# Sums of squares with the squares stationary, one pass for layer 0's two norms, and unsplit fp32 scores in layer 0's attention

## The chip, the cores and the metric

The kernel runs on one core of one Trainium2 chip. The metric is the device time of one execution in microseconds (us). Five engines work side by side: TensorE (PE in the profile, with its weight load PEld), VectorE (DVE), ScalarE (ACT), GpSimd (POOL) and SyncE (SP), which issues most transfers. The granted clock of TensorE (PEclk) is a share of full speed: 1.0 is 2.4 GHz, 0.5 is 1.2 GHz.

## The reference

Two blocks run one behind the other, on 256 tokens of 1024 features in fp32. The first has a state-space mixer, a sparse attention and a mixture of 32 experts, and ends with a norm. The second takes its result as x, has a context of 256 more tokens, and two layers: layer 0 with grouped-query attention (16 heads of 64 for queries, 4 for keys and values), layer 1 with latent attention. Each layer ends with a feed-forward part with a convolution. A norm divides a token by the root of its mean square; the shift and scale behind it come from a vector c ("ada" below):

```
def rms_norm(x, g):
    y = x * lax.rsqrt(jnp.mean(x * x, axis=-1, keepdims=True) + EPS)
    return y * g

def norm_modulate(h, g, shift, scale):
    return rms_norm(h, g) * (1 + scale) + shift
...
def attend(q, k, v):          # layer 0: keys of context and x, 512 in all
    s = jnp.einsum('bqhgd,bkhd->bhgqk', q, k) * scale
    p = softmax_f32(s)
    return jnp.einsum('bhgqk,bkhd->bqhgd', p, v)
```

Where the first block ends, two norms follow each other: x is normed by the block's last gain (final_g), and the result by layer 0's first norm.

## The kernel before

Activations lie feature-major: 128 features on the partitions, 8 tiles of them, 256 tokens along the free dimension. A projection (`lin_fm`, `lin_tm`) splits each fp32 weight into a high and a low part of type fp32r (ScalarE's cast L198, VectorE's difference L199) and makes three fp32r products of them (L217, L218, L219). An fp32r matmul is one record of TensorE in the trace, an fp32 matmul is two.

A norm of x or of the context (`rms_bcast`) has a chain. ScalarE squares two tiles at a time (L484). TensorE sums over features: 8 matmuls with 32 columns of ones stationary, the 256 squares moving, in the four column tiles of 32 (L489). VectorE copies the four partial sums to SBUF (L492), and two matmuls add them up, one column for each half of the tokens (L494). GpSimd takes the power of -1/2 (L507), VectorE puts it on a diagonal (L516), TensorE spreads it over the partitions (L519), VectorE and ScalarE make the scaled activation (L464, L465), which the next projection waits for. `rms_bcast` is called eight times: at the start of the first block; at about 483 us and 503 us for the context's first norm and the router's; at 670 us for the context's feed-forward part, at 1157 us for the context in layer 1; and for x at about 1191, 1407 and 1555 us.

`final_norm` stands where the first block ends (1014 us). It goes through `square_sums` twice, first with h, then with h times the gain (8 squares of ScalarE, L487), and gets the second norm from both (L1417).

In layer 0's attention for x, the queries (16 heads, two on the 128 partitions) and the keys are split into high and low parts as weights are: qTx, khi, klo. A score tile of one head and 128 queries is three fp32r matmuls of 64 rows with 512 keys (L1710); a pair of heads lies in the upper and lower 64 rows. Scores run two steps ahead of their use; between them stand the transposes of the probabilities (L1490) and the products with the values (L1498). VectorE takes the maxima (L1465), divides (L1480) and evicts transposes (L1492); ScalarE makes the exponentials (L1471).

The order of instructions is fixed when the program is built. Generators yield estimated costs, and `weave` and `mix` place a side chain's units among the main chain's by them; buffers of rings ("aux", "lin", "acc", "fl" are PSUM banks) and a planner then set the order on each engine. The ada columns of the second block (L391, `ada_quad`) are placed in this way beside the attention.

The PSUM tiles are called aux for sums of squares, transposes and spreads, lin for projections and scores; sq are squares, XA and the like scaled activations.

Of the kernel before, what the change touches and what calls it, by code (L numbers as in the profile page):

```python
# [88 lines left out]
# The experts by their rank in number of tokens: the order of the units (rank of group, half) and their blocks.  # L89
# [3 lines left out]
# The 8 KB buffers: those of the second part lie where what the first part keeps there is done early.  # L93
# [5 lines left out]
class Kernel:  # L99
# [21 lines left out]
    @contextmanager  # L121
    def banks(self, **bufs):
        """The eight PSUM banks, cut into rings for one part of the program."""
        with self.tc.tile_pool(name="psum", bufs=1, space=bass.MemoryType.PSUM, reuse_waits="tile") as self.psum:
            self.psum_bufs = bufs
            yield

    @contextmanager
    def phase(self, **bufs):
        """Buffers that live for one part of the program."""  # L130
        with self.tc.tile_pool(name="phase", bufs=1, reuse_waits="tile") as p:
            self.phase_pool, self.phase_bufs = p, bufs
# [37 lines left out]
    def passing(self, name, tag):  # L170
        """A constant that is needed only once."""
# [10 lines left out]
    # ---------------------------------------------------------------- weights  # L182
# [5 lines left out]
    def split_weight(self, view):  # L188
        """(hi, lo) of each block of 128 rows of a view [128, n, cols]."""
# [31 lines left out]
    def lin_fm(self, W, c0, ncols, act, evict, k0=0, nk=None, more=False):  # L221
        """out^T: features on partitions. W [K, N] in DRAM; act (hi, lo) [128, nk, 256]."""
# [24 lines left out]
    def lin_tm(self, W, c0, ncols, act, evict, chunk=512):  # L247
        """out: tokens on partitions."""
# [25 lines left out]
    # ---------------------------------------------------------------- set-up  # L274
# [73 lines left out]
    def load_fm(self, src, h, tag, eng):  # L348
        """[256, 1024] rows of DRAM -> feature-major h [128, 8, 256]."""
# [16 lines left out]
    # ---------------------------------------------------------------- adaLN  # L366
# [11 lines left out]
    def take_bias(self, stg, dst):  # L378
        """The bias into dst [128, slots, 48], to which the products are added."""
# [5 lines left out]
    def ada_quad(self, W, q, dst, rsel):  # L385
        """Columns 2048q..2048q+2047 of silu(c) @ W onto dst [128, slots, 48]."""
# [17 lines left out]
    def ada_start(self, p):  # L404
        """Shift and scale of the first norm for half of the features, in the order of ada1."""
# [70 lines left out]
    # ---------------------------------------------------------------- norms  # L476
    def square_sums(self, h, nt, st, gain=None):
        """Sums of squares over features (32 times them) into the two columns of st: the column tiles of TensorE add up
        a quarter each."""
        acc = self.ps("aux", [P, TOK])  # L480
        for k in range(0, nt, 2):
            sq = self.sb("k2", [P, 2, TOK], name="sq")
            if gain is None:
                self.A.activation(sq, h[:, k:k + 2, :], AF.Square)  # L484
            for i in range(2):
                if gain is not None:
                    self.A.activation(sq[:, i, :], h[:, k + i, :], AF.Square, scale=self.v(gain, k + i))  # L487
                c = (k + i) % 4
                self.T.matmul(acc[32 * c:32 * c + 32, :], self.ones[:, 0:32], sq[:, i, :], start=(k < 4),  # L489
                              stop=(k >= nt - 4), skip_group_check=True)  # L490
        part = self.sb("k1", [P, TOK], name="sqsum")
        self.V.tensor_copy(part, acc)  # L492
        for t in range(2):
            self.T.matmul(st[:, t:t + 1], part[:, t * P:t * P + P], self.ones[:, 0:1], start=(t == 0), stop=True,  # L494
                          skip_group_check=True)

    def rms_bcast(self, h, nt, dim):
        """1/rms over features, one column per token, on all partitions (PSUM [128, 256])."""
        st = self.ps("aux", [P, 2])
        self.square_sums(h, nt, st)  # L500
        return self.rstd_bcast(st, 2, 32 * dim)
# [8 lines left out]
    def spread(self, r, n):  # L510
        """Columns of r, one value per token, along the free dimension of all partitions."""
# [11 lines left out]
    def modulation(self, gain, ada, slot, vs, vsc):  # L523
        """gain * (1 + scale) and shift, [128, 8] each."""
# [15 lines left out]
    # ---------------------------------------------------------------- first block: projections  # L540
# [26 lines left out]
    def rope(self, x, nh, t, outs):  # L567
        """x [128, nh, 64] token-major, half-split rotation; written to each of outs."""
# [12 lines left out]
    def project_tm(self, act, pss):  # L581
        """dt, q, k/v, gates of the first block, tokens on partitions; the first two chunks are in pss."""
# [8 lines left out]
    def conv_silu(self, dst, ps, wname, bname, m, nm, taps):  # L591
        """Causal depthwise convolution over tokens, then silu."""
# [20 lines left out]
    # ---------------------------------------------------------------- SSD  # L613
# [40 lines left out]
    def ssd(self):  # L654
        """The chunked scan; y (with the skip) replaces the x channels. Yields where TensorE would wait."""
# [90 lines left out]
    def ssd_gate(self, act, sums):  # L746
        """y * silu(z), and its squares summed by group into sums [2][128, 2, 256]."""
# [35 lines left out]
    # ---------------------------------------------------------------- NSA  # L783
# [141 lines left out]
    def nsa_attend(self):  # L925
        """Selected and window branches (causal both: every block is chosen and the window spans the sequence)."""
# [85 lines left out]
    def tanh_gates(self, act, c0, sg):  # L1012
        """tanh(x / 2): the sigmoid is half of one more."""
# [78 lines left out]
    # ---------------------------------------------------------------- mixture of experts  # L1092
    def router(self, h):
# [35 lines left out]
        def top(x):  # L1129
            """softmax over the 8 columns; its sorted values and their places."""  # L1130
# [55 lines left out]
        # experts by their number of tokens: place of each expert and expert of each place  # L1186
# [67 lines left out]
    def one_hots(self, d, cols):  # L1254
        """For positions 256 d + cols: token x position, by first and second choice, [128, 2, n] per half of tokens."""
# [10 lines left out]
    def expert_gather(self, d, tag, n=256):  # L1266
        """The normalised tokens at positions 256 d.., features on partitions."""
# [15 lines left out]
    def expert_weights(self, part, experts):  # L1283
        """One part of the experts' weights, 256 rows of gate or up or 256 columns of down each."""
# [693 lines left out]
```

## Time and profile before

| what | value |
|---|---|
| runs, device us | 1765.72, 1766.47 (median), 1770.18 |
| profiled execution, span | 1765.9 us |
| TensorE busy | 1690.6 us (96%) |
| its weight load | 1379.4 us (78%) |
| VectorE busy | 1272.3 us (72%) |
| ScalarE busy | 917.8 us (52%) |
| GpSimd busy | 42.4 us (2%) |
| moved by DMA | 381.54 MB, 216 GB/s on average |

The span goes from the first to the last instruction of the profiled execution; no time around it is given apart, and the median of the runs lies 0.6 us above. Busy shares are means over the whole span; a stretch can look quite different. TensorE's ends are modelled: two matmul rows can overlap, and the pace of a row is the distance to the next row's start.

### The profile page before, as it was taken

Reading aid. Unit: us, or ns where it says so; the run is one execution under the profiler, and the core shown is the slowest. Engines: PE = TensorE matmul, PEld = TensorE weight load, DVE = VectorE, ACT = ScalarE, POOL = GpSimd, SP = SyncE. Lnnn points to the kernel's source line nnn. Section 1 sums busy time; section 2 is a strip of 40 time slices with the busy share of each in tenths; the row PEclk is TensorE's granted clock in tenths of the full one; section 3 lists DMA queues with packets and bytes.
Section 4 is the critical chain, followed back from the end, with each engine's and each line's share of the span. In section 5 each row is a group of like instructions: output and inputs, shape, how many; then the busy total and the mean of one; then the engine's idle time right before and its main releaser. Section 6 shows DMA issues by size and latency. Waiting matters only on the chain. (4 is left out here: it accounts for less than half of the span.)

```text
span 1765.9 us, 36466 instructions
## 1 busy us (share of the span) xinstructions
PE 1690.6 (96%) x12980; PEld 1379.4 (78%) x12980; DVE 1272.3 (72%) x3070; ACT 917.8 (52%) x1901; POOL 42.4 (2%) x48
## 2 busy tenths in 40 slices
PE   7999999999999999999999898999999989999998
PEld 3898777767876578888887554688999866789997
DVE  3997687675667768757756466968777788777876
ACT  2666446863443544534434252656665566556654
POOL 0000000100001000000000001000000000000000
PEclk8999999999999999999999988999999999999999
DMA  9756956849966997998999886234566432246662
GB/s 321 212 150 195 322 175 191 253 133 306 317 201 207 323 318 240 329 328 268 325 347 346 258 299 229 90 122 138 178 183 183 141 120 72 59 141 183 180 186 72
DMA packets 344962, 381.54 MB, mean 216 GB/s; under 512 B 27353, under 2 KB 298454, under 8 KB 344774
## 3 DMA queue, kind: packets, MB, share of 16 engines
q1 hardware_dynamic: 339456, 376.47, 67.2%
q10 hardware_dynamic: 5174, 1.97, 0.4%
q8 instruction: 104, 1.70, 0.4%
q0 software_dynamic: 144, 0.71, 0.1%
q14 instruction: 84, 0.69, 0.1%
HBM read 378.00 MB, written 1.05 MB: 215 GB/s over the span
## 5 line engine op out<-in xcount | busy, mean ns | idle before, releaser
L198 ACT CAST whi<-raw 128x512 fp32r<-128x512 f32 (+2 forms) x752 | 453.9, 610 | 383.9 <-PE lin L219 219.5
L199 DVE TENSOR_TENSOR wlo<-raw,whi 128x512 fp32r<-128x512 f32 (+2 forms) x752 | 502.4, 678 | 161.5 <-ACT whi L198 148.6
L217 PE MATMUL lin<-XA,whi 128*128 128x256 f32 x768 | 220.1, 287 | 1.7 <-ACT XA L465 1.7
L219 PE MATMUL lin<-XA,whi 128*128 128x256 f32 x768 | 219.0, 286 | 0.0
L218 PE MATMUL lin<-XA,wlo 128*128 128x256 f32 x768 | 218.9, 285 | 0.0
L217 PE MATMUL lin<-A,whi 128*128 128x256 f32 x576 | 168.4, 292 | 2.7 <-DVE k L598 1.9
L218 PE MATMUL lin<-A,wlo 128*128 128x256 f32 x576 | 163.5, 284 | 0.0
L217 PEld LDWEIGHTS lin<-XA,whi 128*128 128x128 f32 x768 | 149.3, 194 | 2.6 <-ACT XA L465 2.5
L218 PEld LDWEIGHTS lin<-XA,wlo 128*128 128x128 f32 x768 | 149.2, 194 | 0.7 <-issue 0.4
L219 PEld LDWEIGHTS lin<-XA,whi 128*128 128x128 f32 x768 | 148.9, 194 | 0.3
L217 PEld LDWEIGHTS lin<-A,whi 128*128 128x128 f32 x576 | 109.9, 191 | 33.8 <-issue 14.1
L219 PE MATMUL lin<-A,whi 128*128 128x256 f32 x448 | 127.7, 285 | 0.0
L217 PE MATMUL lin<-CA,whi 128*128 128x256 f32 x416 | 122.0, 293 | 0.3 <-ACT whi L198 0.2
L218 PE MATMUL lin<-CA,wlo 128*128 128x256 f32 x416 | 118.2, 284 | 1.1 <-DVE wlo L199 1.1
L219 PE MATMUL lin<-CA,whi 128*128 128x256 f32 x416 | 117.9, 283 | 0.0
L218 PEld LDWEIGHTS lin<-A,wlo 128*128 128x128 f32 x576 | 110.1, 191 | 0.9 <-issue 0.7
L1621 ACT ACTIVATE cv<-lin,vecs 128x256 f32<-128x256 f32 x132 | 73.9, 560 | 63.0 <-PE lin L219 52.7
L219 PE MATMUL lin<-XB,whi 128*128 128x256 f32 x352 | 99.4, 286 | 0.1
L1622 DVE SCALAR_TENSOR_TENSOR cv<-lin,vecs,cv 128x255 f32<-128x255 f32 x132 | 63.3, 480 | 49.4 <-ACT cv L1621 49.1
L217 PE MATMUL lin<-XB,whi 128*128 128x256 f32 x352 | 98.7, 283 | 0.0
L218 PE MATMUL lin<-XB,wlo 128*128 128x256 f32 x352 | 98.4, 283 | 0.0
L217 PEld LDWEIGHTS lin<-CA,whi 128*128 128x128 f32 x416 | 79.2, 190 | 15.5 <-issue 6.5
(534 smaller groups left out, 3835.0 us busy)
## 6 DMA issues: line engine op xcount, KB each, us to landing
raw<-in_ffn_w_up_dram SPq DMA_DIRECT2D x264, 256.0 KB
raw<-in_ada_w_dram SPq DMA_DIRECT2D x192, 256.0 KB
raw<-in_ffn_w_down_dram SPq DMA_DIRECT2D x132, 256.0 KB
raw<-in_w_in_dram SPq DMA_DIRECT2D x112, 256.0 KB
wx<-in_w_exp_gate_dram SPq DMA_DIRECT2D x112, 256.0 KB
wx<-in_w_exp_up_dram SPq DMA_DIRECT2D x112, 256.0 KB
wx<-in_w_exp_down_dram SPq DMA_DIRECT2D x112, 256.0 KB
raw<-in_w_ada_dram SPq DMA_DIRECT2D x96, 256.0 KB
```

The lines of the kernel that those rows point to most:

```text
L198: self.A.copy(hi, raw)
L199: self.V.tensor_tensor(lo, raw, hi.bitcast(F32), OP.subtract)
L217: mm(out, whi, ahi, start=first, stop=False, skip_group_check=True)
L218: mm(out, wlo, ahi, start=False, stop=False, skip_group_check=True)
L219: mm(out, whi, alo, start=False, stop=last, skip_group_check=True)
L1621: A.activation(acc, ps, AF.Identity, bias=self.v(f"fb{i}", m), scale=self.v(f"fw{i}1", m))
L1622: V.scalar_tensor_tensor(acc[:, 1:], ps[:, 0:TOK - 1], self.v(f"fw{i}0", m), acc[:, 1:], OP.mult, OP.add)
```

## The change

`square_sums` lets the squares be stationary: for each tile of features and each half of the tokens one fp32 matmul with 128x128 squares stationary and one or two columns of weights moving, all into one small PSUM tile. The copy (L492) and the two matmuls behind it (L494) are gone. `rms_bcast` takes ones as its one column.

`final_norm` makes one pass with two columns, gain squared plus EPS, and ones, and takes both norms from it. With s1 the mean of h squared and s2 the mean of h squared times gain squared, the second norm needs s2 + EPS (s1 + EPS): the first column's sum, with EPS squared added.

In layer 0's attention the queries and keys stay whole: the scores are one fp32 matmul each (`gqa_S`, which the context's attention had already), ScalarE evicts the queries' transposes, VectorE the keys'. The buffers khi, klo and the second qTx are gone. Comments and docstrings are gone too, so line numbers are lower in the changed kernel: L489 becomes L486, L519 L511, L1710 L1677 (in `gqa_S`), L1490 L1484, L1498 L1492.

```diff
-    def square_sums(self, h, nt, st, gain=None):
-        acc = self.ps("aux", [P, TOK])
-        for k in range(0, nt, 2):
+    def square_sums(self, h, weights, n):
+        st = self.ps("aux", [P, 2, n])
+        for k in range(0, 8, 2):
             sq = self.sb("k2", [P, 2, TOK], name="sq")
-            if gain is None:
-                self.A.activation(sq, h[:, k:k + 2, :], AF.Square)
+            self.A.activation(sq, h[:, k:k + 2, :], AF.Square)
             for i in range(2):
-                if gain is not None:
-                    self.A.activation(sq[:, i, :], h[:, k + i, :], AF.Square, scale=self.v(gain, k + i))
-                c = (k + i) % 4
-                self.T.matmul(acc[32 * c:32 * c + 32, :], self.ones[:, 0:32], sq[:, i, :], start=(k < 4),
-                              stop=(k >= nt - 4), skip_group_check=True)
-        part = self.sb("k1", [P, TOK], name="sqsum")
-        self.V.tensor_copy(part, acc)
-        for t in range(2):
-            self.T.matmul(st[:, t:t + 1], part[:, t * P:t * P + P], self.ones[:, 0:1], start=(t == 0), stop=True,
-                          skip_group_check=True)
+                for t in range(2):
+                    self.T.matmul(st[:, t, :], sq[:, i, t * P:t * P + P], weights(k + i), start=(k + i + t == 0),
+                                  stop=(k + i == 7), skip_group_check=True)
+        return st
...
     def rms_bcast(self, h, nt, dim):
-        st = self.ps("aux", [P, 2])
-        self.square_sums(h, nt, st)
-        return self.rstd_bcast(st, 2, 32 * dim)
+        st = self.square_sums(h, lambda k: self.ones[:, 0:1], 1)
+        return self.rstd_bcast(st.rearrange("p t n -> p (t n)"), 2, dim)
...
     def final_norm(self, h, gain, mod, tag):
-        count = 32 * D
-        st = [self.ps("aux", [P, 2]) for _ in range(2)]
-        self.square_sums(h, 8, st[0])
+        w = self.sb("s", [P, 8, 2])
+        V.tensor_tensor(w[:, :, 0], self.v(gain, 0, 8), self.v(gain, 0, 8), OP.mult)
+        V.tensor_scalar(w[:, :, 0], w[:, :, 0], EPS, None, OP.add)
+        V.memset(w[:, :, 1], 1.0)
+        st = self.square_sums(h, lambda k: w[:, k, :], 2)
         ms = self.sb("s", [P, 2, 2])
-        V.tensor_scalar(ms[:, 0, :], st[0], 1.0 / count, EPS, OP.mult, OP.add)
-        self.square_sums(h, 8, st[1], gain)
-        V.scalar_tensor_tensor(ms[:, 1, :], ms[:, 0, :], EPS * count, st[1], OP.mult, OP.add)
+        V.tensor_scalar(ms[:, 0, :], st[:, :, 0], 1.0 / D, EPS * EPS, OP.mult, OP.add)
...
         def take(t, c0, tp):
-            if not is_x:
...
-            elif c0 == 1024:
-                self.evict_split(*[k[:, :, TOK + t * P:TOK + t * P + P] for k in kT], tp)
+            if c0 == 1024:
+                k0 = (TOK if is_x else 0) + t * P
+                V.tensor_copy(kT[:, :, k0:k0 + P], tp)
             else:
-                self.evict_split(*[q[:, c0 // P:c0 // P + 4, t * P:t * P + P] for q in qT], tp)
+                A.copy(qT[:, c0 // P:c0 // P + 4, t * P:t * P + P], tp)
...
     def layer0_x_attend(self):
-        qT = [self.sb(n, [P, 8, TOK], F32R, name="qTx") for n in ("Q", "CA0")]
-        klo = self.sb("CA1", [P, 4, 512], F32R, name="klo")
...
-        def S_fn(S, i, t):
-            (qh, ql), (kh, kl) = [[x[:, i, t * P:t * P + P] for x in qT], [x[:, i // 2, :] for x in kT]]
-            for n, (q, k) in enumerate(((qh, kh), (ql, kh), (qh, kl))):
-                for a in range(2):
-                    r = slice(64 * a, 64 * a + 64)
-                    self.T.matmul(S[a], q[r], k[r], start=(n == 0), stop=(n == 2))
+        qT = self.sb("Q", [P, 8, TOK], name="qTx")
+        kT = self.kT2
+        S_fn = self.gqa_S(qT, 4)
```

At layer 0's two norms the order on TensorE was this in the kernel before (L489 the four column tiles' products, L494 their sums, L519 the spread, L391 products for ada, L217 and L218 projections):

```order
5004 L489 MATMUL aux<-sq,ones 32x256 x8
5005 L494 MATMUL aux<-ones,sqsum 128x1 x2
5006 L489 MATMUL aux<-sq,ones 32x256 x4
5007 L391 MATMUL fl<-raw,stat 32x512
5008 L489 MATMUL aux<-sq,ones 32x256 x4
5009 L391 MATMUL fl<-raw,stat 32x512 x2
5010 L494 MATMUL aux<-ones,sqsum 128x1 x2
5011 L391 MATMUL fl<-raw,stat 32x512
5012 L519 MATMUL aux<-k_14529,ones 128x256
5013 L391 MATMUL fl<-raw,stat 32x512 x2
5014 L217 MATMUL lin<-whi,XA_14533 128x512 x2
```

The first pass's sums stand between the two passes, and ada products among the second.

In the changed kernel the same place reads (L486 the new products, L511 the spread):

```order
5006 L486 MATMUL aux<-s,sq 128x2 x16
5007 L511 MATMUL aux<-k_14522,ones 128x256
5008 L391 MATMUL fl<-raw,stat 32x512
5009 L217 MATMUL lin<-whi,XA_14526 128x512 x2
5010 L391 MATMUL fl<-raw,stat 32x512
5011 L218 MATMUL lin<-whi,XA_14527 128x512
```

The two passes with ada products among them have become one run of 16 matmuls, and the ada products stand behind the spread.

In layer 0's attention, one period of the scores on TensorE before (L1490 transposes of probabilities, L1710 scores, L1498 and its second half products with the values):

```order
5203 L1490 MATMUL aux<-ident,prob 128x128 x8
5204 L1710 MATMUL lin<-khi,qTx 128x512 x4
5205 L1710 MATMUL lin<-klo,qTx 128x512 x2
5206 L1710 MATMUL lin<-khi,qTx 128x512 x2
5207 L1710 MATMUL lin<-klo,qTx 128x512
5208 L1490 MATMUL aux<-ident,prob 128x128 x8
5209 L1710 MATMUL lin<-khi,qTx 128x512 x2
5210 L1710 MATMUL lin<-klo,qTx 128x512
5211 L1498 MATMUL acc<-pT,vc 64x256 x4
5212 L1498 MATMUL acc<-pT,vx 64x256 x4
```

Four heads' scores stand in two places, three of them together.

And after (L1484 transposes, L1677 scores, L1492 products with the values):

```order
5200 L1484 MATMUL aux<-ident,prob 128x128 x8
5201 L1677 MATMUL lin<-kT_6574,qTx 128x512 x2
5202 L1484 MATMUL aux<-ident,prob 128x128 x8
5203 L1677 MATMUL lin<-kT_6574,qTx 128x512
5204 L1492 MATMUL acc<-pT,vc 64x256 x4
5205 L1492 MATMUL acc<-pT,vx 64x256 x4
5206 L1677 MATMUL lin<-kT_6574,qTx 128x512
5207 L1484 MATMUL aux<-ident,prob 128x128 x8
5208 L1677 MATMUL lin<-kT_6574,qTx 128x512 x2
5209 L391 MATMUL fl<-raw,stat 32x512 x3
```

Before, a period has the scores of a pair of heads, of a single head right behind it, and of another single head behind the next transposes; after, a pair and two single heads, one on each side of the products with the values.

## Rows read from the trace of the kernel before

**Rows 1.** Windows: us, busy time of PE, PEld, DVE, ACT, POOL, PEclk, DMA share, GB/s.

```profile
690.00:720.00 30.00, 30.00 (x287) 25.81 (x286) 21.35 (x47) 14.38 (x27) 0.00 (x0) 1.00 0.99 317
1011.00:1028.30 17.30, 12.76 (x52) 4.56 (x54) 5.33 (x15) 8.74 (x19) 1.66 (x2) 0.51 0.69 235
1108.66:1135.16 26.50, 26.50 (x177) 16.86 (x176) 25.56 (x65) 17.99 (x47) 0.00 (x0) 1.00 0.26 84
1560.00:1568.00 8.00, 6.89 (x33) 6.36 (x32) 6.62 (x16) 4.14 (x9) 0.00 (x0) 0.57 0.00 0
```

**Rows 2.** Time line of PE, router: start, us, line, out<-in, form, count.

```profile
517.67 2.20 PE L1114 MATMUL aux<-wr,hn 128*128 128x36 f32 x18
519.80 0.62 PE L391 MATMUL acc<-raw,stat 128*32 128x512 f32 x1
```

**Rows 3.** Time line of PE, the context's norm ahead of its feed-forward part.

```profile
670.13 1.07 PE L489 MATMUL aux<-sq,ones 128*32 128x256 f32 x16
671.13 1.13 PE L1317 MATMUL acc<-raw,xg 128*128 128x256 f32 x4
672.10 0.50 PE L494 MATMUL aux<-ones,sqsum 128*128 128x1 f32 x4
672.46 1.97 PE L1317 MATMUL acc<-raw,xg 128*128 128x256 f32 x8
```

**Rows 4.** Time line of PE, x's norm ahead of layer 1's feed-forward part.

```profile
1554.60 1.06 PE L489 MATMUL aux<-sq,ones 128*32 128x256 f32 x12
1556.30 0.63 PE L489 MATMUL aux<-sq,ones 128*32 128x256 f32 x4 [0.64 <-ACT sq L484]
1557.45 0.61 PE L494 MATMUL aux<-ones,sqsum 128*128 128x1 f32 x4 [0.53 <-DVE sqsum L492]
1559.73 0.67 PE L519 MATMUL aux<-k,ones 128*128 128x256 f32 x2 [1.67 <-DVE k L516]
```

**Rows 5.** Time line of PE, layer 0's two norms.

```profile
1014.88 2.62 PE L489 MATMUL aux<-sq,ones 128*32 128x256 f32 x16 [4.22 <-ACT sq L484]
1018.04 1.01 PE L494 MATMUL aux<-ones,sqsum 128*128 128x1 f32 x4 [0.53 <-DVE sqsum L492]
1018.98 1.08 PE L489 MATMUL aux<-sq,ones 128*32 128x256 f32 x8
...
1023.42 1.01 PE L494 MATMUL aux<-ones,sqsum 128*128 128x1 f32 x4
...
1028.83 0.50 PE L217 MATMUL lin<-whi,XA 128*128 128x512 f32 x1
```

**Rows 6.** Time line of PE, one period of layer 0's attention.

```profile
1118.18 0.73 PE L1710 MATMUL lin<-khi,qTx 64*128 64x512 f32 x4
...
1120.00 1.09 PE L1490 MATMUL aux<-ident,prob 128*128 128x128 f32 x8
1121.02 0.73 PE L1710 MATMUL lin<-khi,qTx 64*128 64x512 f32 x2
...
1121.91 0.44 PE L1498 MATMUL acc<-pT,vc 128*64 128x256 f32 x2
```

**Rows 7.** Time line of PE, fp32 scores of the first block.

```profile
336.41 1.13 PE L941 MATMUL S<-kT,qT 64*128 64x512 f32 x4
337.47 0.39 PE L217 MATMUL lin<-A,whi 128*128 128x256 f32 x1
```

**Rows 8.** Time line of PE, fp32 scores of the context's attention.

```profile
574.89 0.70 PE L1687 MATMUL S<-kT,qTc 64*128 64x256 f32 x4
...
599.56 0.70 PE L1687 MATMUL S<-kT,qTc 64*128 64x256 f32 x2
```

**Rows 9.** Time line of PE, projections and transposes ahead of layer 0's attention.

```profile
1064.02 0.39 PE L217 MATMUL lin<-whi,XA 128*128 128x512 f32 x1
1064.24 0.39 PE L218 MATMUL lin<-whi,XA 128*128 128x512 f32 x1
...
1067.91 0.63 PE L1571 MATMUL aux<-ident,pr 128*128 128x128 f32 x4 [2.08 <-DVE pr L1448]
```

More of the change, by code (lines that the diff above doesn't have):

```diff
@@ L1409, in final_norm @@
         a, b = mod
-        count = 32 * D
-        st = [self.ps("aux", [P, 2]) for _ in range(2)]
-        self.square_sums(h, 8, st[0])
+        w = self.sb("s", [P, 8, 2])
[3 more added lines that the diff above has]
+        st = self.square_sums(h, lambda k: w[:, k, :], 2)
         ms = self.sb("s", [P, 2, 2])
-        V.tensor_scalar(ms[:, 0, :], st[0], 1.0 / count, EPS, OP.mult, OP.add)
-        self.square_sums(h, 8, st[1], gain)
-        V.scalar_tensor_tensor(ms[:, 1, :], ms[:, 0, :], EPS * count, st[1], OP.mult, OP.add)
+        V.tensor_scalar(ms[:, 0, :], st[:, :, 0], 1.0 / D, EPS * EPS, OP.mult, OP.add)
         r = self.sb("s", [P, 2])
-        self.G.tensor_tensor(r, ms[:, 1, :], self.mhalf[:, 0:2], OP.pow)
+        self.G.tensor_tensor(r, ms[:, 0, :], self.mhalf[:, 0:2], OP.pow)
+        V.tensor_scalar(ms[:, 1, :], st[:, :, 1], 1.0 / D, EPS, OP.mult, OP.add)
         ag = self.sb("s", [P, 8])
-        V.scalar_tensor_tensor(ag, a, count ** 0.5, self.v(gain, 0, 8), OP.mult, OP.mult)
+        V.tensor_tensor(ag, a, self.v(gain, 0, 8), OP.mult)
         rb = self.spread(r, 2)
@@ L1425, in final_norm @@
         r1 = self.sb("s", [P, 2])
-        self.G.tensor_tensor(r1, ms[:, 0, :], self.mhalf[:, 0:2], OP.pow)
+        self.G.tensor_tensor(r1, ms[:, 1, :], self.mhalf[:, 0:2], OP.pow)
         def scale():
@@ L1586, in take @@
         def take(t, c0, tp):
-            if not is_x:
-                if c0 == 1024:
-                    V.tensor_copy(kT[:, :, t * P:t * P + P], tp)
-                else:
-                    A.copy(qT[:, c0 // P:c0 // P + 4, t * P:t * P + P], tp)
-            elif c0 == 1024:
-                self.evict_split(*[k[:, :, TOK + t * P:TOK + t * P + P] for k in kT], tp)
+            if c0 == 1024:
+                k0 = (TOK if is_x else 0) + t * P
+                V.tensor_copy(kT[:, :, k0:k0 + P], tp)
             else:
-                self.evict_split(*[q[:, c0 // P:c0 // P + 4, t * P:t * P + P] for q in qT], tp)
+                A.copy(qT[:, c0 // P:c0 // P + 4, t * P:t * P + P], tp)
         W = self.I["gqa_w_in_2"][0]
@@ L1692, in layer0_x_attend @@
         act, scale = self.final_norm(h, "final", self.mods(self.ada2[0], 0, "n1_0", 0), "XA")
-        qT = [self.sb(n, [P, 8, TOK], F32R, name="qTx") for n in ("Q", "CA0")]
-        klo = self.sb("CA1", [P, 4, 512], F32R, name="klo")
-        his = []
-        for g in range(0, 4, 2):
-            hi = self.sb("k2", [P, 2, TOK], F32R, name="khi")
-            self.evict_split(hi, klo[:, g:g + 2, 0:TOK], self.kT2[:, g:g + 2, 0:TOK])
-            his.append(hi)
-        khi = self.sb("K", [P, 4, 512], F32R, name="khi")
-        for g in range(0, 4, 2):
-            self.A.copy(khi[:, g:g + 2, 0:TOK], his[g // 2].bitcast(F32))
-        kT = khi, klo
-        def S_fn(S, i, t):
-            (qh, ql), (kh, kl) = [[x[:, i, t * P:t * P + P] for x in qT], [x[:, i // 2, :] for x in kT]]
-            for n, (q, k) in enumerate(((qh, kh), (ql, kh), (qh, kl))):
-                for a in range(2):
-                    r = slice(64 * a, 64 * a + 64)
-                    self.T.matmul(S[a], q[r], k[r], start=(n == 0), stop=(n == 2))
+        qT = self.sb("Q", [P, 8, TOK], name="qTx")
+        kT = self.kT2
+        S_fn = self.gqa_S(qT, 4)
         self.gqa_rope_tables()
```

## The prediction

> **What bounds the kernel now.** I read the stretches by engine first [rows 1], then the time line of TensorE where the change touches it, then the waits. In rows 1 the reader sees TensorE busy for all 30 us of 690 to 720 and all 26.5 us of the attention stretch 1108.66 to 1135.16. Two other engines stand close behind: the DMA engines are full in the first (share 0.99), VectorE in the second (25.56 of 26.50 us). So work added to TensorE shows in the end unless one of those two was late anyway. At the norms it is different: TensorE waits there, and afterwards the granted clock is low, 0.51 from 1011 to 1028.3 and 0.57 from 1560 to 1568 (most of it at 1.2 GHz, the rest at 2.4). There the chain from squares to the scaled activation sets the time.
>
> My sum is made against the profiled span, 1765.9 us. The median of the runs, 1766.47, lies 0.6 us above it, and I add that at the end. A change of less than 0.3% (5.3 us) can't be told from none.
>
> **The products of the norms.** Each call loses 8 matmuls with 32 stationary columns, one VectorE copy and two matmuls with the sum stationary. It gains 16 matmuls, each with its own 128x128 fp32 stationary and one or two moving columns. An fp32 matmul is two records. The nearest row is the router's product, 128x128 stationary and 36 moving columns: 18 records from 517.67, the next row starts at 519.80, so with its change-over 0.118 us a record [rows 2]. The 16 matmuls are 32 records: about 3.7 us at the full clock. What they replace is seen whole at the context's norm ahead of its feed-forward part: 1.00 us from 670.13 to 671.13, and 0.36 us from 672.10 to 672.46 [rows 3], 1.36 us in all. The four column tiles worked at once there. The price is +2.3 us of TensorE a call.
>
> The Trainium skill, "TensorE: Matmul & The Clock Gate", has two sections that price this differently. "Back-to-back issue gap" gives some 25 ns between matmuls of 1 to 64 columns; by that alone a call would be 0.8 us, cheaper than before (an estimate from the page). "LDWEIGHTS (loading the stationary operand)" gives columns over 1.2, thus 107 ns for 128 columns whatever the rows; by that a call is 3.4 us (an estimate too). The router's row, far above 25 ns, agrees with the second, and its 36 columns are no more than the first speaks of.
>
> Where does the +2.3 us count? Nine calls:
> - Four stand in full streams of TensorE (the context's first norm, the router's, the context's before its feed-forward part in layer 0, the context's in layer 1). Bounds: 0 each, if the transfers or a later wait take it up, and 2.3 each. The one at 670 stands right before the stretch with DMA share 0.99, so a later start there may be made up; the others have no such cover close behind. I take 1.3 each: +5.2, bounds 0 and +9.2.
> - Three are x's norms with TensorE waiting. In the one at 1554.60 the products waited for the last squares until 1556.30, then for the copy until 1557.45, and the last ended at 1557.45 + 0.61 = 1558.06 [rows 4]. The new ones run through: 1554.60 + 32 x 0.118 = 1558.38, with the end of the last about 0.1 later. The copy's wait of 0.53 and the squares' 0.64 are eaten by the backlog. +0.4 each, +1.2; bounds -0.6 each (if only the last pair of features is left when its squares come) and +1 each.
> - The first call lies where weights are still arriving: 0, bounds -0.5 and +0.5.
> - The last is the shared one of layer 0, below.
>
> **Layer 0's two norms.** Before, two passes go one behind the other: products from 1014.88, the sums of the first at 1018.04, the second's at 1023.42 + 1.01 = 1024.43, all at the low clock [rows 5]; then come the power on GpSimd, the spread and the first projection at 1028.83 [rows 5]. After, one pass of 32 records. At this clock the same kind of matmul takes 0.94 / 4 = 0.235 us a record (1018.04 to 1018.98) [rows 5]: 1014.88 + 7.5 = 1022.4, 2.0 us earlier. The eight scaled squares on ScalarE go too, and behind the power nothing changes. At the full clock 32 records would end 3.7 us earlier still; if the clock came back later because the stretch has less work in it, the gain would be 0. I take -2.0, bounds -5.7 and 0.
>
> **The scores of layer 0.** Before, a pair of heads is 6 records of fp32r, a single head 3. In one period of the attention there is a pair and a single from 1118.18 to 1120.00 and a single from 1121.02 to 1121.91: 1.82 + 0.89 = 2.71 us for four heads [rows 6]. Unsplit, a pair of 64-row heads with 512 keys is 4 records; the first block has the same shape in 1.06 us (336.41 to 337.47) [rows 7]. What one head alone costs is not in the trace with 512 keys; with 256 keys a single head lasts as long as a pair, 0.70 and 0.70 [rows 8], since the pair's row groups work side by side. So a single is 1.06 too. It now matters how the heads stand: the order puts pairs, and singles with other products between them. From the order's row 5183 on there are 24 heads in 7 pairs and 10 singles: 17 x 1.06 = 18.0 us. Before, 24 heads at 2.71 for four, the first pair at 0.9: 0.9 + 5.5 x 2.71 = 15.8 us. +2.2 us, bounds -3.1 (all 12 in pairs: 12.7) and +3.2 (another 0.1 for each change-over). TensorE was full there, so it counts. VectorE, at 25.56 of 26.50 us, loses nothing within that stretch, so it doesn't let the stretch get shorter either; it loses the low parts of q and k before it, 8 operations, and ScalarE as many. That lies beside TensorE's work and I count it at nothing; were it on the path, the q parts (two on the way to each four pairs of heads) could give back up to 1.4 us.
>
> **Moved.** The transposes of the first query heads stand behind 17 rather than 24 projections of the next chunk. Before, TensorE waited 2.08 us for them [rows 9]. Such a projection takes 0.22 us (1064.02 to 1064.24) [rows 9]; reached 7 of them earlier, 1.5 us, the transposes may wait as much longer, and what is behind them waits too; some of that is made up by the shorter norm ahead. +0.5, bounds 0 and +1.5. Before the attention is full, one head's scores now go ahead of 12 projections, and the softmax's start moves with them; the two sides about cancel: 0, bounds -2 and +2. The ada products that stand between them are the same in number.
>
> **Sum.** 5.2 + 1.2 + 0 - 2.0 + 2.2 + 0.5 = +7.1: a span of 1773.0, a median of 1773.6. I say 1773.5.
>
> **Rivals.**
> 1. The waits at the norms end and the clock stays up. In favour: the low clock after x's norm follows waits of 0.64, 0.53 and 1.67 us [rows 4], and the first two go. A mean of 0.57 over 8 us is 6.9 us at the lower level [rows 1], of which 3.4 would come back; for three such norms, taken as alike, 10.2, and 3.7 in the shared norm: 13.9, thus 1759.6, faster. It decides as soon as two stretches stay up and the shared norm runs at the full clock. Against it: from 1011 to 1028.3 TensorE worked 12.76 of 17.3 us and the clock stayed low [rows 1], so narrow work did not lift it there. Chance 0.15.
> 2. The additions are hidden. The four full calls are made up behind transfers and the scores stand as in the old order's bound: 7.1 - 5.2 - 1 = +0.9, thus 1767.4. For it: DMA share 0.99 and VectorE at 25.56 of 26.50 [rows 1]. Against: TensorE is busy 30.00 of 30 in the same rows, so nothing there stands idle to take it. Chance 0.30.
> 3. The products run at the pace of narrow matmuls, as if the load of the stationary cost nothing. (The Trainium skill, "TensorE: Matmul & The Clock Gate", "Back-to-back issue gap", would have them quicker still.) By rows: at the pace of the old ones, 16 records in 1.00 us [rows 3], 32 would be 2.0, +0.6 a call: 4 x 0.4 in the full streams, -0.6 at each of x's norms, -4.3 in the shared one (16 records took 2.62 us from 1014.88 [rows 5], so 32 end at 1020.1), +2.2 and +0.5: -1.8, thus 1764.7. Against: rows 2. Chance 0.05.
> 4. The clock falls more: 32 records of one column leave the array nearly empty, and each of x's three norms and the shared one has half as much time again at half speed (3.4 us, costing 1.7): +6.8, thus 1780.3. Chance 0.10.
>
> The forecast has 0.40. Below 1761.2 lies most of rival 1 (0.13); between 1761.2 and 1771.8 are rivals 2 and 3, the rest of rival 1 and the lower edge of the forecast (0.41); above, most of the forecast and rival 4 (0.46). The range runs from 1762 (both low bounds of full calls and scores: 1773.5 - 5.2 - 5.3 = 1763, and some of rival 1) to 1783 (9.2, the moved transposes at 1.5, and one more low clock stretch).
>
> **What would show it.** The new products at 0.12 us a record, 3.7 us a call: right; at 0.06 or less, rival 3. The single fp32 scores at 1.06: right; at 0.55, the scores gain. The first projection of layer 0 at about 2 us less after the products' start than the 13.95 us before. A granted clock of 1.0 after x's norms would be rival 1, and the time from 690 to 1011 growing shorter by what came before it, rival 2. I am wrong if the median is below 1771.8, and the sign is wrong below 1766.

## The result, and the profile after

The changed kernel takes 1786.5 us (median of 4 runs, 1783.98 to 1789.04), the kernel before in the same runs 1766.1. The ratio is 1.0108, 95% interval [1.0091, 1.0126]: 16 to 22 us slower, some 19 in the middle. I had forecast slower, by 7.1 us, with a range to 1783. So the sign was right and the size wrong by a factor of nearly three. The profiled execution has a span of 1787.3 us; the casts of the weights (L198) serve as marks along both traces, and the distance between them grows in four steps: 4.4 us by 100 us (an expectation below has it as 5.1), 10.4 by 660 us, 15.2 by 980 us, 20.6 to 21.4 from 1200 us to the end.

The time line of TensorE at the context's norm ahead of its feed-forward part answers to [rows 3], that at x's last norm to [rows 4], at layer 0's two norms to [rows 5] and in the attention to [rows 6]:

```profile
680.41 3.72 PE L486 MATMUL aux<-ones,sq 128*128 128x1 f32 x32
684.00 2.05 PE L1309 MATMUL acc<-raw,xg 128*128 128x256 f32 x4
...
1029.22 0.80 PE L486 MATMUL aux<-s,sq 128*128 128x2 f32 x3 [4.38 <-ACT sq L483]
1031.77 6.14 PE L486 MATMUL aux<-s,sq 128*128 128x2 f32 x29 [1.75 <-issue]
1039.58 1.19 PE L511 MATMUL aux<-k,ones 128*128 128x256 f32 x2 [1.68 <-DVE k L508]
1040.70 1.92 PE L391 MATMUL fl<-raw,stat 128*32 128x512 f32 x2
1042.55 1.22 PE L217 MATMUL lin<-whi,XA 128*128 128x512 f32 x2
...
1137.87 1.13 PE L1677 MATMUL lin<-kT,qTx 64*128 64x512 f32 x4
1138.93 1.09 PE L1484 MATMUL aux<-ident,prob 128*128 128x128 f32 x8
1139.96 1.12 PE L1677 MATMUL lin<-kT,qTx 64*128 64x512 f32 x2
1141.03 1.08 PE L1492 MATMUL acc<-pT,vc 128*64 128x256 f32 x8
...
1575.18 3.98 PE L486 MATMUL aux<-ones,sq 128*128 128x1 f32 x32
1580.83 1.19 PE L511 MATMUL aux<-k,ones 128*128 128x256 f32 x2 [1.67 <-DVE k L508]
```

The prices are as forecast. The 32 records take 684.00 - 680.41 = 3.59 us, 0.112 each, against 1.36 us for what they replace [rows 3]. A pair of heads takes 1138.93 - 1137.87 = 1.06 us, a single one 1141.03 - 1139.96 = 1.07. What was not in my sum at these norms stands behind the products. The windows give the time, the busy time of PE, PEld, DVE, ACT and POOL, the granted clock, the DMA share and GB/s; of each pair, the first ends with the products (at the context's first norm 16 of the 32 records, with projections among them) and the second is what follows:

```profile
489.60:492.80 3.20, 3.20 (x30) 3.20 (x30) 0.16 (x2) 0.62 (x1) 0.00 (x0) 1.00 0.66 244
492.80:496.20 3.40, 3.40 (x17) 3.22 (x16) 2.17 (x7) 1.15 (x2) 1.13 (x1) 0.51 0.29 78
...
680.40:684.00 3.60, 3.60 (x35) 3.60 (x33) 0.00 (x0) 1.62 (x3) 0.00 (x0) 1.00 0.00 0
684.00:687.40 3.40, 3.40 (x10) 2.53 (x10) 1.83 (x8) 0.00 (x0) 0.70 (x1) 0.50 0.07 9
```

TensorE is busy all through both pairs and waits for nothing, and yet the clock is at 1.2 GHz behind the products. In the kernel before it was at 2.4 GHz at these places:

```profile
480.00:500.00 20.00, 19.66 (x159) 17.51 (x158) 16.79 (x38) 12.37 (x24) 0.72 (x1) 1.00 0.61 204
500.00:520.00 20.00, 18.70 (x124) 12.16 (x123) 9.10 (x22) 7.18 (x15) 0.70 (x1) 1.00 0.58 171
660.00:680.00 20.00, 19.71 (x149) 17.67 (x148) 14.70 (x35) 7.65 (x16) 1.05 (x1) 1.00 0.59 187
```

The clock falls like this behind the context's first norm, with the router's last products (513 to 520 us), behind the context's norm before its feed-forward part, and once more in layer 1.

The two traces also tell where the scores cost: from the first product with the values to the last, TensorE needed 46.98 us before (the first two rows) and 51.27 after (the last two):

```profile
1108.66 0.65 PE L1498 MATMUL acc<-pT,vc 128*64 128x256 f32 x4
...
1155.64 1.24 PE L1498 MATMUL acc<-pT,vx 128*64 128x256 f32 x7
...
1120.51 1.08 PE L1492 MATMUL acc<-pT,vc 128*64 128x256 f32 x8
...
1171.78 1.24 PE L1492 MATMUL acc<-pT,vx 128*64 128x256 f32 x7
```

That is +4.3 us. By the distance of starts, the scores of the 22 heads in this stretch take 17.2 us for 14.0, and six records of ada products (L391), 1.0 us, stand inside it now, where there were none. But the first product with the values lay only 11.85 us behind the kernel before, 2.5 us less than at the first product of layer 0's norms (1014.88 to 1029.22, 14.3 us).

### The profile page after: what moved, and what is told of

Read it like the earlier page. It is cut to its first block, busy times and chain, and to the rows that moved or that the text cites. A ratio compares the mean times of both kernels' runs of the same rounds, so it can differ in the third digit from the quotient of the medians.

```text
span 1787.3 us, 36539 instructions
## 1 busy us (share of the span) xinstructions
PE 1716.0 (96%) x13036; PEld 1405.6 (79%) x13036; DVE 1267.3 (71%) x3057; ACT 912.9 (51%) x1887; POOL 42.0 (2%) x48
## 5 line engine op out<-in xcount | busy, mean ns | idle before, releaser
L198 ACT CAST whi<-raw 128x512 fp32r<-128x512 f32 (+2 forms) x752 | 454.0, 610 | 396.8 <-PE lin L219 228.0
L199 DVE TENSOR_TENSOR wlo<-raw,whi 128x512 fp32r<-128x512 f32 (+2 forms) x752 | 503.0, 679 | 168.0 <-ACT whi L198 153.0
L217 PE MATMUL lin<-XA,whi 128*128 128x256 f32 x768 | 220.0, 287 | 1.6 <-ACT XA L465 1.6
L218 PE MATMUL lin<-XA,wlo 128*128 128x256 f32 x768 | 218.8, 285 | 0.0
L217 PE MATMUL lin<-A,whi 128*128 128x256 f32 x576 | 168.4, 292 | 2.7 <-DVE k L590 1.9
L218 PE MATMUL lin<-A,wlo 128*128 128x256 f32 x576 | 163.5, 284 | 0.0
L217 PEld LDWEIGHTS lin<-XA,whi 128*128 128x128 f32 x768 | 149.3, 194 | 2.9 <-ACT XA L465 2.7
L218 PEld LDWEIGHTS lin<-XA,wlo 128*128 128x128 f32 x768 | 149.1, 194 | 0.6 <-issue 0.4
L217 PEld LDWEIGHTS lin<-A,whi 128*128 128x128 f32 x576 | 109.9, 191 | 33.8 <-issue 14.1
L217 PE MATMUL lin<-CA,whi 128*128 128x256 f32 x416 | 122.1, 294 | 0.2 <-ACT whi L198 0.2
L218 PE MATMUL lin<-CA,wlo 128*128 128x256 f32 x416 | 117.9, 283 | 1.1 <-DVE wlo L199 1.1
L218 PEld LDWEIGHTS lin<-A,wlo 128*128 128x128 f32 x576 | 110.1, 191 | 0.9 <-issue 0.7
L217 PE MATMUL lin<-XB,whi 128*128 128x256 f32 x352 | 98.7, 283 | 0.0
L218 PE MATMUL lin<-XB,wlo 128*128 128x256 f32 x352 | 98.4, 283 | 0.0
L217 PEld LDWEIGHTS lin<-CA,whi 128*128 128x128 f32 x416 | 79.3, 191 | 15.2 <-issue 7.0
```

Of the source, the lines that this page charges most:

```text
L198: self.A.copy(hi, raw)
L199: self.V.tensor_tensor(lo, raw, hi.bitcast(F32), OP.subtract)
L217: mm(out, whi, ahi, start=first, stop=False, skip_group_check=True)
L218: mm(out, wlo, ahi, start=False, stop=False, skip_group_check=True)
```

## The experiments

Each was timed in five rounds beside the kernel before, on one chip for each group of four or three kernels. A ratio is that to the kernel before, with its 95% interval, and microseconds are ratio minus one times its median (1767.5 to 1768.4 us in these runs).

**Scores or norms.** The first kernel is the kernel before with `layer0_x_attend` and `take` of the change, the second the kernel before with `square_sums`, `rms_bcast` and `final_norm` of the change.

> The kernel before with unsplit fp32 scores alone; all norms as before. Theory A (the new products of the norms make the loss): between 0 and +4 us against before, from +4.3 us in the full part of the attention and -2.4 us ahead of it, as the two traces differ there. Theory B (the scores are the main loss, by singles at 1.06 us and what they delay): +8 us or more.

> The kernel before with the new sums of squares in all nine calls and the shared pass; scores split as before. Theory A: +16 to +20 us, most of it at five calls in full streams (the first, the context's first, the router's, the context's two others), and a low granted clock after each of them. Theory B: +8 us or less.

Measured: 0.9996 [0.998, 1.0011] for the scores, -0.7 us; 1.0103 [1.0073, 1.0133] for the norms, +18 us. Within these intervals the whole loss is in the norms. In the scores' own trace the first product with the values starts at 1101.89, 6.8 us earlier than before, and the last at 1153.16, 2.5 us earlier: the +4.3 us inside the full attention is there again (as in all four profiles with unsplit scores), and made up ahead of it. What went ahead of it was not one wait: the transposes' 2.1 us [rows 9] and part of the low clock, which took 10.2 us from 1082.8 in the kernel before and 3.4 us at about that place here. The latter can't be put down to the scores: in the profiles of kernels that are as before in this part, that stretch is between 0 and 10.2 us long.

**Which norms.** `rms_bcast` takes the new sums in some of its calls only; the kernel with the shared norm has the change's `final_norm` instead:

```diff
     def rms_bcast(self, h, nt, dim):
+        self.calls = getattr(self, "calls", -1) + 1
+        if self.calls in (1, 2, 3, 4):      # (5, 6, 7) and (0,) in the others
+            st = self.square_sums_new(h, lambda k: self.ones[:, 0:1], 1)
+            return self.rstd_bcast(st.rearrange("p t n -> p (t n)"), 2, dim)
         st = self.ps("aux", [P, 2])
         self.square_sums(h, nt, st)
```

> The kernel before with the new sums of squares in four plain norms alone, those in TensorE's full streams (the context's first norm, the router's, the context's before its feed-forward part in layer 0, the context's in layer 1). Theory A (each costs 2.3 us of records, and the low clock behind it 1.7 us or more again): +11 to +15 us. Theory B (my prediction's price, 1.3 us each, the rest hidden): +5 us.

> The kernel before with the new sums of squares in x's three plain norms alone. Theory A: 0 to +2 us, since the products there run beside waits and the copy's chain goes. Rival: the low clock behind them gets longer, as in the changed kernel's trace (10.2 us in place of 6.8 at two of them), and they cost +3 us or more.

> The kernel before with the new sums of squares in the first norm alone (at 16 us). Theory A (its records on a full TensorE and the order that comes with it): +4 to +6 us, as the changed kernel lies 5.1 us behind by 100 us. Theory B (the start is bound by weights arriving, as I predicted): within 1 us of before.

> The kernel before with layer 0's two norms shared as in the change (squares stationary, two columns moving), nothing else. My prediction's term: -2.0 us, bounds -5.7 and 0. Rival from the changed kernel's trace, where the chain from the first square to the first projection took 14.0 us against 14.6: within 1 us of before.

| new sums in | ratio | interval | us |
|---|---|---|---|
| the four full streams | 1.0047 | [1.0033, 1.006] | +8.3 |
| x's three norms | 1.0013 | [1.0004, 1.0023] | +2.3 |
| the first norm | 1.004 | [1.0024, 1.0055] | +7.1 |
| layer 0's shared norm | 1.0012 | [1.0, 1.0023] | +2.1 |

The four add up to 19.8 us, the kernel with all of them had +18. So one call in nine, the first, costs nearly as much as the four in the full streams. These cost less than the +11 to +15 us that I expected then: the trace has +6.8 us behind the first two and another 3.3 us behind the third by 705 us, of which 1.0 is made up by 980 us and 4.1 more by 1150 us; the fourth adds 1.1 by 1190 us.

Why is the shared norm no gain? In this kernel its chain is shorter, as I forecast: 11.57 us from the first product to the first projection, where the ten profiles with the old norms and split scores here have 12.3 to 14.1. In its time line the last product of the experts starts at 1010.59, 0.90 us later than before, and the first projection 1.84 us earlier than [rows 5]:

```profile
1015.42 6.99 PE L506 MATMUL aux<-s,sq 128*128 128x2 f32 x32 [3.85 <-ACT sq L503]
1023.99 1.22 PE L535 MATMUL aux<-k,ones 128*128 128x256 f32 x2 [1.58 <-DVE k L532]
1025.13 1.92 PE L391 MATMUL fl<-raw,stat 128*32 128x512 f32 x4
1026.99 0.97 PE L217 MATMUL lin<-whi,XA 128*128 128x512 f32 x2
...
1078.51 0.73 PE L1729 MATMUL lin<-khi,qTx 64*128 64x512 f32 x4
```

But the first scores start at 1078.51, in the kernel before at 1078.34. The gain is gone in the projections: from the first of them to the first scores it is 51.5 us, and 48.2 to 50.4 in those ten. In the kernel before 12 records of ada products (L391) stood among the second pass, up to the first projection, and used its waits; here 4 stand ahead of it and the other 8 among the projections, where TensorE is full. Between the first projection and the first scores there are 60 such records now and 52 before; by the distance of starts they take 10.9 us for 9.2, and TensorE's waits there are 3.1 us for 2.3. That accounts for the gain in these two time lines; I didn't run a kernel that keeps the ada products back. In the changed kernel the chain gained less to begin with: TensorE stands still for 1.75 us behind the first three records (1029.22 and 1031.77 above), and the first projection comes 13.33 us behind the first product, against 13.95. What held it there the profile doesn't tell (`issue`).

**The low clock behind the products.** One norm alone (the context's in layer 1) takes the new sums, with 1, 36 and 128 columns of ones moving. TensorE's order is the same in the three, row by row.

```diff
-            st = self.square_sums_new(h, lambda k: self.ones[:, 0:1], 1)
-            return self.rstd_bcast(st.rearrange("p t n -> p (t n)"), 2, dim)
+            st = self.square_sums_new(h, lambda k: self.ones[:, 0:36], 36)
+            return self.rstd_bcast(st[:, :, 0], 2, dim)
```

> The kernel before with the new sums of squares in one plain norm alone, the context's in layer 1 (at 1157 us). Theory A: +2.3 us of records and 1.7 us for a stretch of low clock behind them: +3 to +5 us in the trace behind the norm. Theory B (records alone): +2.3 us.

> As the kernel with one new norm, with 36 columns of ones moving in place of one; TensorE's order is otherwise the same row by row. Theory A (the clock falls for the single column): the products take the same time, the granted clock stays at 1.0 behind them, and 1.7 us or more come back. Theory B: the same as with one column.

> As the kernel with one new norm (the context's in layer 1), with 128 columns of ones moving; TensorE's order is otherwise the same row by row. If the low clock behind the products comes from how little moves through TensorE, 128 columns keep it at 1.0 and the kernel is within 2 us of before plus the records' 2.3 us; if it comes from the stationary loads or from the stretch itself, the granted clock falls again right behind the products as with 1 and 36 columns.

Measured: 1.0019 [1.0006, 1.0032], 1.0016 [1.0004, 1.0028] and 1.0017 [1.0005, 1.003], so +3 us for each. The time lines of the products and, in the same order, the windows behind them:

```profile
1157.12 3.63 PE L506 MATMUL aux<-ones,sq 128*128 128x1 f32 x32
1160.61 0.36 PE L217 MATMUL lin<-CB,whi 128*128 128x256 f32 x1
```

```profile
1158.28 3.82 PE L506 MATMUL aux<-ones,sq 128*128 128x36 f32 x32
1161.91 0.56 PE L217 MATMUL lin<-CB,whi 128*128 128x256 f32 x1
```

```profile
1153.78 3.73 PE L506 MATMUL aux<-ones,sq 128*128 128x128 f32 x32
1157.27 0.36 PE L217 MATMUL lin<-CB,whi 128*128 128x256 f32 x1
```

```profile
1161.10:1164.50 3.40, 3.33 (x14) 2.89 (x14) 1.90 (x5) 0.03 (x1) 0.69 (x1) 0.51 0.13 38
```

```profile
1161.60:1165.00 3.40, 3.40 (x16) 3.17 (x15) 0.68 (x4) 0.00 (x0) 0.70 (x1) 0.50 0.07 24
```

```profile
1157.50:1161.00 3.50, 2.81 (x23) 2.58 (x22) 1.80 (x6) 0.67 (x2) 0.69 (x1) 1.00 0.00 1
```

The products take 3.49, 3.63 and 3.49 us, whatever moves: the loads of the stationary set their pace. Behind them the clock is low with 1 and with 36 columns and stays up with 128. So Theory A fell for 36 columns, and the time did not follow the clock here. In these profiles the low clock came earlier and not on top: with 128 columns, and in the kernel before, a stretch of 3.4 us begins later, at 1168.7 and 1171.6, behind a wait of TensorE for a weight's low part (L199) of 2.1 and 2.71 us, and with 1 and 36 columns there is none at that place, though TensorE waits 2.1 us there too. The windows of the kernel before, of that with 128 columns and of that with one (clock third from the end):

```profile
1172.00:1180.00 8.00, 8.00 (x57) 8.00 (x56) 3.71 (x8) 3.19 (x7) 0.00 (x0) 0.81 0.74 237
```

```profile
1165.00:1172.00 7.00, 4.68 (x24) 4.35 (x23) 5.95 (x13) 3.57 (x7) 0.00 (x0) 0.76 0.40 119
```

```profile
1165.00:1172.00 7.00, 4.72 (x37) 4.29 (x36) 6.48 (x17) 4.87 (x12) 0.00 (x0) 1.00 0.01 3
1172.00:1180.00 8.00, 7.96 (x64) 7.96 (x65) 5.47 (x11) 4.05 (x9) 0.00 (x0) 1.00 0.79 245
```

From 1155 to 1190 us the three time lines lose 1.3, 1.1 and 1.9 us against the kernel before. The +3 us agree with that and with the records' 2.1 to 2.3, within their intervals.

The same edit in all eight plain norms of the changed kernel:

> The changed kernel with 36 columns of ones moving instead of one in the eight plain norms, nothing else. Theory A1 (the clock falls because one-column matmuls leave TensorE nearly without work, though it is busy by the record): records at the same 0.11 us, the clock stays at 1.0 behind the context's norm ahead of its feed-forward part, and 4 to 9 us of the loss come back. Theory A2 (the clock falls for what stands around, or the time is lost by the records alone): no change, within 2 us of the changed kernel.

Measured: 1.0056 [1.0032, 1.0079], +10 us, so about half of the loss is gone. That looked like Theory A1, but with 36 columns the planner also gave TensorE another order. In the trace 3.9 of the 4.4 us of the start are gone, and 3.6 more by 720 us, where the clock is low for 3.4 us behind the context's first norm and not at all at the two next (13.6 us in the changed kernel at these three). There too some rows stand in another order, so this kernel doesn't part the clock from the order.

**The first norm: clock or order.** With 36 columns its products stand in two blocks of eight instead of four of four, and there are fewer ada products (L412) between the first projections. The kernels with 16 and 24 columns have about as much moving, but the first keeps the order of the one-column kernel around the first projections, the second that of the 36-column kernel. One piece of the difference on TensorE around the first projections, with - for 16 columns and + for 24:

```order
 L419 MATMUL aux<-ident,rowt 128x128 x2
-L412 MATMUL fl<-raw,stat 32x256
+L412 MATMUL fl<-raw,stat 32x256 x4
 L217 MATMUL lin<-whi,A_172 128x468 x2
-L412 MATMUL fl<-raw,stat 32x256 x3
 L218 MATMUL lin<-whi,A_173 128x468 x2
```

The ada products now stand ahead of the first projection's products.

> As the kernel with the new sums in the first norm alone, with 36 columns moving. The products then stand in two blocks of eight in place of four of four, and the first projections with fewer ada products among them. Theory A (records): the same +4 to +6 us, for the records are as many and as long. Theory B (the order of the ada products around them): within 1 us of before, as the trace of the kernel with 36 columns in all norms stood only 0.5 us behind by 100 us.

> As the kernel with the new sums in the first norm alone, with 16 columns moving. From the transposes ahead of the first projection on, TensorE's order is that of the one-column kernel (ada products between the first projections). Theory order: +5 us or more, as with one column. Theory columns (the clock): well below that, towards the 36-column kernel's +1.4 us.

> As the last, with 24 columns moving. From the transposes ahead of the first projection on, TensorE's order is that of the 36-column kernel. Theory order: near +1.4 us. Theory columns: about the same as with 16 columns.

| columns, order | ratio | interval | us | clock, DMA share of 22 to 38 us | SyncE waited for L412 |
|---|---|---|---|---|---|
| 1, between | 1.004 | [1.0024, 1.0055] | +7.1 | 0.57, 0.76 | 7.0 us |
| 16, between | 1.0024 | [1.0007, 1.004] | +4.2 | 0.89, 0.91 | 6.2 us |
| 24, ahead | 1.0006 | [0.9992, 1.0019] | +1.1 | 0.79, 0.98 | 3.0 us |
| 36, ahead | 1.0008 | [0.9994, 1.0021] | +1.4 | 1.00, 1.00 | 1.6 us |
| kernel before | | | | 0.70, 1.02 | 4.6 us |

The windows from 22 to 38 us of the kernel before, of that with one column and of that with 36 (clock, DMA share and GB/s at the end of the row):

```profile
22.00:38.00 16.00, 15.36 (x86) 7.30 (x87) 7.10 (x19) 4.87 (x11) 0.00 (x0) 0.70 1.02 370
```

```profile
22.00:38.00 16.00, 14.24 (x62) 5.59 (x61) 7.72 (x21) 4.15 (x9) 0.72 (x1) 0.57 0.76 268
```

```profile
22.00:38.00 16.00, 13.39 (x102) 6.19 (x97) 7.65 (x20) 4.29 (x10) 0.23 (x1) 1.00 1.00 358
```

And the waits of SyncE's queue for the ada products, in the same order (in all, times, the longest):

```profile
SPq L185 <- PE fl L412: 4.6, 9, 1.2
```

```profile
SPq L185 <- PE fl L412: 7.0, 6, 3.7
```

```profile
SPq L185 <- PE fl L412: 1.6, 5, 0.4
```

The start is bound by transfers: in the kernel before the 16 DMA engines are full. With one column SyncE waits up to 3.7 us at once for an ada product to free a weight buffer, and the DMA share falls to 0.76: 0.26 of 16 us are 4.2 us of lost transfer. With the ada products ahead, SyncE waits 3.0 or 1.6 us in all, and the loss is within what can be measured, although the products are as many and as long.

The last two columns of the table come from one profile each; the other profiles of this study say how far they can be trusted. Ten kernels have the old first norm, that before among them. In their profiles SyncE waits 1.4 to 4.6 us for L412, the DMA share is 0.95 to 1.03, and by 100 us they lie between 0.5 us ahead of and 2.0 us behind the kernel before. The low clock takes 0 to 10.2 us there, the most in the kernel before, and the time doesn't follow it. Three profiles have one column (this kernel, the changed one, the norms alone): all have 13.7 us of low clock, waits of 7.0 to 8.5 us, and lie 4.4 to 5.2 us behind by 100 us. With 16 columns it is 2.6 us, and in the three with the ada products ahead (24, 36, and 36 in all eight norms) between -0.5 and +1.9.

The order is thus the larger part; but the intervals of 16 and 24 columns overlap, those of 1 and 16 as well, and between 1 and 16 columns, where the order is alike from there on, 2.9 us and a clock of 0.57 against 0.89 remain. How much of the 7.1 us is the clock stays open.

**The shared norm with column tiles.** Layer 0's two norms share their squares, but the sums keep 32 stationary columns and the four column tiles:

```diff
-        self.square_sums(h, 8, st[0])
...
+        acc = self.ps("aux", [P, 2, TOK])
+        for k in range(0, 8, 2):
+            sq = self.sb("k2", [P, 2, TOK], name="sq")
+            self.A.activation(sq, h[:, k:k + 2, :], AF.Square)
+            for i in range(2):
+                c = (k + i) % 4
+                for j, st in enumerate((w[:, k + i, :], self.ones[:, 0:32])):
+                    self.T.matmul(acc[32 * c:32 * c + 32, j, :], st, sq[:, i, :], start=(k < 4 and j == 0),
+                                  stop=(k >= 4), skip_group_check=True)
```

> The kernel before, with layer 0's two norms from one set of squares as in the change, but summed with 32 stationary columns in the four column tiles, once with ones and once with gain squared. Theory: the second set of squares (3.3 us of ScalarE) and the second chain go, and the products keep their pace: -3 to -5 us against before. Rival: the chain is bound by the low clock and the waits behind it, and it gains less than 1 us, as the changed kernel's shared pass did.

> The unsplit scores and the shared norm in column tiles together, the eight plain norms as before. Theory: the shared norm's gain stays (-1 to -3 us) and the scores add nothing: -1 to -4 us against before. Rival: the scores' +4.3 us in the full attention is no longer made up ahead of it, since the shared norm has taken that gain: 0 to +3 us.

Measured: 0.9987 [0.9974, 0.9999], -2.3 us, and with the unsplit scores 0.9999 [0.9985, 1.0013]. The first is the fastest kernel of this study, by little, and short of the 3 to 5 us I expected. Its first projection comes 4.45 us earlier than before (1024.38), the first product with the values 2.5 us (1106.11): TensorE waits 2.35 us for low parts of weights (L199) among the projections in place of 0.22. The two together gain nothing that can be measured; the interval, -2.7 to +2.3 us, leaves room for the second's theory as well as for its rival. The rival's reason, that the shared norm has taken what made up for the scores, is not shown by a run of its own.

## Why the prediction was wrong

- **The first norm** is the step that failed: "The first call lies where weights are still arriving: 0, bounds -0.5 and +0.5". It measured +7.1 us. Arriving weights are no cover when TensorE has to free their buffers: SyncE waited for L412 in the kernel before too (4.6 us there, 1.4 to 2.8 in nine other profiles with the old norm). With the new one it waited 7.0 us, and the DMA share fell from 1.02 to 0.76. How much of that is the order of the ada products and how much the clock stays open. I had no row on it and did not ask what queues behind a late TensorE.
- **The four full streams** were mis-sized, +8.3 us for +5.2, within the bounds of 0 and 9.2. The records cost 2.1 to 2.3 us, as worked out. I left out the low clock behind them, which I had only in rival 4 and there for the wrong norms, x's; in the trace of these four it is 6.8, 6.8 and 3.4 us long behind the first three, 8.5 us if all of it counted. The trace has 10.1 us behind these three, 3.4 more than the records. Part is made up, as rival 2 had it: 1.0 us among the experts, 4.1 more by 1150 us.
- **x's norms**: +2.3 us for +1.2, within the measurement of it (+0.7 to +4.1). At the last, the products end at 1575.18 + 3.98, 0.5 us later after their start than the old sums [rows 4]. The waits behind are the same 1.67 us.
- **The shared norm**: +2.1 us for -2.0. Alone, the chain from the experts' last product got shorter by 2.7 us, so the working held up to the first projection; in the changed kernel it gained 0.6 from the products' start. That "behind the power nothing changes" was false: the order shown ahead of the prediction has the ada products behind the spread.
- **Scores and what was moved**: -0.7 us for +2.7. The single head at 1.06 us is right, and the attention's full part got 4.3 us longer where I had 2.2: 3.2 for the scores, and 1.0 for ada products that came into this stretch, for which my sum had nothing. What I left at 0, the way there, gave back as much.

The sum of the measured terms, 7.1 + 8.3 + 2.3 + 2.1 - 0.7 = 19.1, is what the change measured. The measured median also lies above the range's end of 1783, and the parts that I named for that end come to 1780.2 only. Rival 1 did not come: the stretch of low clock behind x's norms got no shorter, and was 10.2 us long behind two of them. The Trainium skill, "TensorE: Matmul & The Clock Gate", section "LDWEIGHTS (loading the stationary operand)", has the columns over 1.2, thus some 107 ns for a load of 128 columns (an estimate from the page); the trace agrees, with 0.109 to 0.113 us a record for 1, 36 and 128 moving columns. The 25 ns in the table of its "Back-to-back issue gap" are the gap of an isolated matmul, which by that section is too little at few columns, since the load of the stationary isn't in it; I took them as a rival price for such a stream, and here it was 0.112 us with one column and a stationary for each matmul.

## What to carry to other kernels

A matmul whose stationary operand is used once costs the load, here 0.11 us for each of two records in fp32, and making the data stationary to save a copy turned 1.4 us into 3.6. Where a stretch is bound by transfers, ask which engine frees the buffers, since delaying that one delays the transfers; one call at such a place cost nearly as much as four elsewhere. When an edit shortens a chain with waits in it, look for what used to run in the waits: it doesn't vanish with them.

## What the hardware showed

I did not expect the granted clock to fall while TensorE was busy without a gap. Behind 3.5 us of products with a fresh 128x128 stationary each, it was 0.51 with one moving column and 0.50 with 36, for 3.4 us, and 1.00 with 128, at the same pace of records. Over all profiles, the clock fell during or right behind such products in full streams 13 times of 13 with one column, 3 of 5 with 36, and not at the one place with 128. Nor did I expect a matmul with 128 moving columns to cost no more than one with a single column: 3.49 us for 32 records either way.
